# Values in two halves of their columns, VectorE's steps issued when ScalarE's results are made, and the mixer's gate behind six tiles of queries and keys

## The chip, the cores and the metric

The kernel runs on one core of a Trainium2 chip. The metric is the device time of one execution in microseconds (us), less is better. TensorE multiplies matrices, VectorE and ScalarE work element by element, GpSimd (POOL in the profile) does a few additions, SyncE (SP) issues the DMAs.

## The reference

Two layers of a decoder trunk over 512 positions of width 1024. Each layer has two half-step feed-forward blocks, between them a token mixer, and behind them a per-layer embedding. The change lies in the mixer:

```python
a_in = rms_norm(h, mix_pre_g[i])
proj = a_in @ w_in[i]
q, k, v, u = jnp.split(proj, [D_ATTN, 2 * D_ATTN, 3 * D_ATTN], axis=-1)
q = partial_rotary(...); k = partial_rotary(...)          # 8 heads of 64
attn = dilated_mixture_attention(q, k, v)                 # windows (128,1) (512,4) (2048,16)
ssm = s5_mixer(u, ...)                                    # 32 groups of 16 channels, 64 states
mixed = jnp.concatenate([rms_norm(attn, attn_norm_g[i]), rms_norm(ssm, ssm_norm_g[i])], axis=-1)
h = h + rms_norm(mixed @ w_out[i], mix_post_g[i])
# the end of s5_mixer:
y = jax.nn.gelu(y)
y = y * jax.nn.sigmoid(y @ w_glu + b_glu)
```

All of it is float32, and the sequence is one batch of 512 positions.

## The kernel before

Activations lie with channels on the 128 partitions and the 512 positions along the free axis. A product with weights is done in three passes of a rounded format: each operand is split into a high half (ScalarE copies it, which rounds) and a low half (VectorE subtracts), and `mm3` (line 632) multiplies high by high, high by low and low by high. The weights come as units of 128 x 1024 words, in the order that `weight_units` (line 84) lists; `splitter` (line 694) splits a unit ahead of its use, up to two ahead, and `take` (line 712) forces it if it is not there. Raw units are loaded three ahead by DMAs on SP's queue.

Every engine runs its instructions in the order in which the program issues them. That order is made by a planner: `Clock` (line 203) keeps a modelled time for each engine, and work off the main line is written as generators that yield the modelled time at which they want to go on. `ck.after(ns)` waits for so much modelled time after TensorE's, `ck.written(ap)` is the modelled time at which an area is written, `ck.ready` the time at which TensorE may read it, `ck.idle("DVE")` the time at which VectorE has nothing left. The main line issues matmuls; before each step (`step`, line 967) it lets all generators go on whose time has come. None of these is a wait of the hardware: they only set what stands before what in each engine's queue. Real waits are semaphores of the data.

The mixer is `mix` (line 1821). First six units (`HEAD`, line 49) are multiplied: four of u, the input of the state-space part, and the query and key tiles of the first two heads (a head pair, t = 0). Then the main line multiplies the values (lines 1886 to 1900): four units hold two blocks of 128 input channels each and all 512 value columns, and four PSUM banks, one for each block of 128 positions, gather over all units, so that no values are there before the end of the fourth. Then come the other six query and key tiles, two to a head pair, with the gate `glu` (line 1941) ahead of tile `GLU_AT` = 4 (line 51), which counts the two in `HEAD`: two tiles, the gate, four tiles. Then the output projection's state-space half, which needs the four normalised pairs `xs`, and its attention half, which needs all attention.

Beside the main line run: two lanes of `mixer` (line 1559), each with two of four octets of groups; `attention` (line 1778), at most three `block`s (line 1686) at a time, one per head pair and 128 queries, whose second product reads the values (line 1740 waits for all four); `parts` (line 1751), which makes the rounded halves of a head pair in six slots of the 36 (`NR`, line 43); `attended` (line 1798), which ends a head pair. The end of an octet is its GELU: ScalarE's Square, two VectorE steps, ScalarE's Tanh, a VectorE step, a split into two rounded slots (lines 1662 to 1673). `glu` waits in the planner until both lanes are done, does four tiles of matmuls, and issues after each at once Tanh, the VectorE product and the sum of squares; its `scale` then waits for the norm and makes the four pairs, with a pause for an idle VectorE behind each (line 1977).

The profile names nearly all instructions by the helper's line (616 and 629 for matmuls, 379 for the others), so rows are told apart by engine, operation and tile shape.

## Time and profile before

| | us |
|---|---|
| median of 3 runs | 2089.26 |
| lowest and highest | 2086.16, 2090.63 |
| the profiled execution | 2087.56 |
| its span, first to last instruction | 2085.8 |
| TensorE (PE) busy in it | 2030.9 |
| VectorE (DVE) busy | 1329.9 |
| ScalarE (ACT) busy | 807.0 |
| GpSimd (POOL) busy | 156.4 |

Busy time of a matmul is modelled, and matmuls overlap, so a busy TensorE is not one at its peak. PEclk is the clock that TensorE was granted, as a share of 2.4 GHz. A row of the timeline gives start, duration, engine, line, operation, what it writes and reads, shape and count; in brackets the idle time of the engine before it and what ended that. A row that merges several instructions shows the first one's shape.

### The profile page before, as it was taken

What the parts mean: (1) busy time and instruction counts of PE and PEld (TensorE: products, weight loads), DVE (VectorE), ACT (ScalarE), POOL (GpSimd) and SP (SyncE); (2) the same over time, 40 slices, a digit from 0 to 9 for tenths busy, and PEclk for the clock granted to TensorE, in tenths of its full rate; (3) what the DMA queues carried; (4) which work ended last, traced back from release to release, by engine and by line L of the source; (5) the groups of instructions that cost most, each with busy time, mean ns of one, the idle gap of its engine ahead of it and who ended that gap; (6) DMA issues with size and microseconds to landing.
All of it is one profiled execution on the core that took longest, in us unless ns stands there. A gap on an engine that the chain in (4) does not pass through costs nothing.

```text
span 2085.8 us, 30582 instructions
## 1 busy us (share of the span) xinstructions
PE 2030.9 (97%) x11864; PEld 1745.4 (84%) x11864; DVE 1329.9 (64%) x2516; ACT 807.0 (39%) x1406; POOL 156.4 (8%) x167
## 2 busy tenths in 40 slices
PE   7999999997999999999999999999999999999997
PEld 7888888985789888888998888889777988888897
DVE  6886654777778867445774444458877854445474
ACT  4422332444654333223553222234457543222253
POOL 0000000210220000001210000011011200000022
PEclk9999999999999999999999999999999999999999
DMA  5434342482233434424324233243812433323132
GB/s 162 126 95 147 107 140 91 155 183 63 81 114 114 155 105 131 136 64 159 112 78 145 63 114 107 76 158 122 183 52 71 141 113 98 114 71 123 60 131 72
DMA packets 118145, 236.29 MB, mean 113 GB/s; under 512 B 27120, under 2 KB 58480, under 8 KB 118000
## 3 DMA queue, kind: packets, MB, share of 16 engines
q1 hardware_dynamic: 118000, 234.34, 36.5%
q8 instruction: 93, 1.52, 0.3%
q14 instruction: 52, 0.43, 0.1%
HBM read 208.60 MB, written 25.69 MB: 112 GB/s over the span
## 4 chain that ended last, share of the span: by engine, by line
PE 88%; DVE 7%; ACT 2%; DMA 2%; issue 1%; SPq 0%; POOL 0%; DVEq 0%; ACTq 0%; POOLq 0%
PE ps_all L616 87%; DVE sb_all L379 4%; DVE sr_all L379 2%; PE ps_all L629 1%; ACT sb_all L379 1%; ACT sr_all L379 1%; DMA sb_all<-scratch_g 1%; DMA sb_all<-scratch_t 1%; SPq L379 0%; DMA sb_all<-xt 0%; DMA z<-scratch_t 0%; DVE z L379 0%; POOL sb_all L379 0%; ACT z L379 0%; DVEq L379 0%
## 5 line engine op out<-in xcount | busy, mean ns | idle before, releaser
L616 PE MATMUL ps_all<-sr_all 128*128 128x512 f32 (+1 forms) x7259 | 1421.6, 353 | 21.5 <-ACT sr_all L379 18.6
L616 PEld LDWEIGHTS ps_all<-sr_all 128*128 128x128 f32 x7259 | 1191.6, 190 | 209.0 <-ACT sr_all L379 20.4
L379 ACT ACTIVATE sr_all<-sb_all 128x1024 fp32r<-128x1024 f32 (+5 forms) x570 | 414.8, 744 | 593.1 <-DVE sb_all L379 432.1
L379 DVE TENSOR_TENSOR sr_all<-sb_all,sr_all 128x1024 fp32r<-128x1024 f32 (+4 forms) x458 | 422.1, 931 | 205.6 <-ACT sr_all L379 204.0
L616 PE MATMUL ps_all<-sr_all,z 128*128 128x512 f32 (+1 forms) x2757 | 547.4, 350 | 2.0 <-DVE sr_all L379 2.0
L616 PEld LDWEIGHTS ps_all<-sr_all,z 128*128 128x128 f32 x2757 | 452.0, 190 | 68.5 <-DVE sr_all L379 3.0
L379 DVE TENSOR_TENSOR sb_all<-ps_all,sb_all 128x512 f32<-128x512 f32 (+1 forms) x400 | 246.9, 622 | 325.1 <-PE ps_all L616 316.9
L379 ACT ACTIVATE sb_all<-sb_all 128x256 f32<-128x256 f32 (+3 forms) x388 | 187.6, 491 | 451.4 <-DVE sb_all L379 451.1
L379 POOL TENSOR_TENSOR sb_all<-sb_all 128x256 f32<-128x256 f32 (+3 forms) x159 | 152.7, 962 | 1924.5 <-ACT sb_all L379 1726.6
L379 DVE TENSOR_TENSOR sb_all<-sb_all 128x256 f32<-128x256 f32 (+7 forms) x605 | 238.3, 410 | 52.4 <-DMA scratch_t<-sb_all 37.2
L379 ACT ACTIVATE sb_all<-ps_all 128x512 f32<-128x512 f32 (+5 forms) x215 | 102.7, 492 | 165.2 <-PE ps_all L616 123.2
L379 DVE SCALAR_TENSOR_TENSOR sb_all<-sb_all 128x512 f32<-128x512 f32 (+3 forms) x194 | 115.1, 595 | 52.9 <-ACT sb_all L379 51.1
L379 DVE TENSOR_TENSOR z<-sb_all,z 128x1024 fp32r<-128x1024 f32 (+2 forms) x109 | 116.3, 1069 | 46.5 <-ACT z L379 46.2
L379 ACT ACTIVATE z<-sb_all 128x1024 fp32r<-128x1024 f32 (+2 forms) x109 | 100.4, 924 | 54.3 <-PE ps_all L616 37.7
L616 PEld LDWEIGHTS ps_all<-sb_all 128*64 128x64 f32 (+3 forms) x1364 | 76.6, 145 | 36.1 <-DVE sb_all L379 12.4
L616 PE MATMUL ps_all<-sb_all 128*64 128x128 f32 (+5 forms) x1364 | 88.8, 257 | 17.1 <-DVE sb_all L379 8.5
L379 DVE SCALAR_TENSOR_TENSOR sb_all<-sb_all,ps_all 128x256 f32<-128x256 f32 (+1 forms) x136 | 65.8, 485 | 4.4 <-ACT sb_all L379 2.8
L379 DVE TENSOR_SCALAR sb_all<-sb_all 128x32 f32<-128x32 f32 (+8 forms) x145 | 41.7, 296 | 29.6 <-POOL sb_all L379 17.0
L379 DVE SCALAR_TENSOR_TENSOR sr_all<-sb_all,sr_all 128x256 fp32r<-128x256 f32 x96 | 51.1, 543 | 0.4 <-ACT sr_all L379 0.4
L629 PE MATMUL ps_all<-sb_all 128*128 128x128 f32 x278 | 45.7, 279 | 5.0 <-DVE sb_all L379 3.8
L629 PEld LDWEIGHTS ps_all<-sb_all 128*128 128x128 f32 x278 | 33.2, 140 | 14.3 <-DVE sb_all L379 7.0
L379 DVE CUSTOM_DVE_ANT_0 sb_all<-ps_all,sb_all 128x512 f32<-128x512 f32 (+3 forms) x56 | 24.7, 491 | 16.5 <-PE ps_all L616 16.5
(36 smaller groups left out, 168.8 us busy)
## 6 DMA issues: line engine op xcount, KB each, us to landing
sb_all<-weights SPq DMA_DIRECT2D x263, 512.0 KB, 3.6
sb_all<-weights SPq DMA_DIRECT2D x96, 320.0 KB, 3.0
scratch_t<-sb_all SPq DMA_DIRECT2D x40, 256.0 KB, 3.8
scratch_h<-sb_all SPq DMA_DIRECT2D x80, 128.0 KB, 1.7
sb_all<-scratch_h SPq DMA_DIRECT2D x40, 256.0 KB, 5.5
sb_all<-scratch_t SPq DMA_DIRECT2D x16, 512.0 KB, 6.3
sb_all<-weights SPq DMA_DIRECT2D x32, 192.0 KB, 2.3
sb_all<-xt SPq DMA_DIRECT2D x16, 128.0 KB, 3.8
```

The costliest lines, as they stand in the source:

```text
L379: return f(*a, **k)
L616: self.nc.tensor.matmul(out, lhsT, rhs, start=start, stop=stop)
L629: self.nc.tensor.transpose(out, x, self.ident)
```

## The change

Values: a unit now holds four blocks of input channels and half of the value columns; for each half two units are taken, and each block of positions is summed up in one bank over eight steps of 256 columns and evicted at once. An attention block waits only for the half that its head pair needs. `GLU_AT` goes from 4 to 6: four query and key tiles stand ahead of the gate and two behind it, and the weight units are ordered to match. In the GELU, in `attended` and in the gate, VectorE steps that read a ScalarE result are issued when the planner holds it to be written. The gate's element-wise steps become a generator per tile. `scale` works in place, issues ScalarE's rounding of one tile before VectorE's subtraction of the tile before it, and has no pause.

```diff
-GLU_AT = 4
+GLU_AT = 6
@@ lay_out
         elif name == "w_in" and how == "v":
-            b = w[t * 2 * P:(t + 1) * 2 * P, 2 * DA:3 * DA].reshape(2, P, DA).transpose(1, 0, 2)
+            c = 2 * DA + t // 2 * HALF
+            b = w[t % 2 * 4 * P:(t % 2 + 1) * 4 * P, c:c + HALF].reshape(4, P, HALF).transpose(1, 0, 2)
@@ mixer
             self.act(gw, ps, AF.Square)
+            yield self.ck.written(gw)
             self.ts(gw, gw, 0.044715, 1.0, ALU.mult, ALU.add)
             self.tt(gw, ps, gw)
             self.act(gw, gw, AF.Tanh, scale=math.sqrt(2 / math.pi))
-            yield self.ck.after(500.0)
+            yield self.ck.written(gw)
             self.stt(self.b(g), gw, 1.0, ps, ALU.add, ALU.mult)
@@ block
-        while len(M["have"]) < 4:
+        while t // 2 not in M["have"]:
             yield self.ck.after(200.0)
-        yield self.ck.ready(*pt, *[self.b(x) for x in v])
+        yield self.ck.ready(*pt, *[self.b(x)[:, t * P:(t + 1) * P] for x in v])
@@ attended
         self.sumsq(self.b(M["sqa"]), ps, t == 0)
+        yield self.ck.written(self.r(h))
         self.stt(self.r(l), ps, g, self.r(h).bitcast(F32), ALU.mult, ALU.subtract)
@@ mix
-        bks = [self.bank() for _ in range(4)]
-        for j in range(4):
-            u, = self.take("w_in")
-            for kk in range(2):
-                k = 2 * j + kk
-                c = slice(kk * SEQ, (kk + 1) * SEQ)
-                for t in range(4):
-                    s = slice(t * P, (t + 1) * P)
-                    self.step(self.pb(bks[t]), (self.r(x["H"][k]), self.r(x["L"][k])), s,
-                              u[0][:, c], u[1][:, c], k, KT)
-            self.done()
-        for t in range(4):
-            self.act(self.b(v[t]), self.pb(bks[t]), scale=x["rt"][:, t:t + 1])
-            self.free(bks[t])
-            have.append(t)
+        for half in range(2):
+            u = self.take("w_in", 2)
+            for t in range(4):
+                bk = self.bank()
+                s = slice(t * P, (t + 1) * P)
+                for k in range(KT):
+                    c = slice(k % 4 * HALF, (k % 4 + 1) * HALF)
+                    self.step(self.pb(bk, HALF), (self.r(x["H"][k]), self.r(x["L"][k])), s,
+                              u[k // 4][0][:, c], u[k // 4][1][:, c], k, KT)
+                    if t == 3 and k % 4 == 3:
+                        self.done()
+                self.act(self.b(v[t])[:, half * HALF:(half + 1) * HALF], self.pb(bk, HALF), scale=x["rt"][:, t:t + 1])
+                self.free(bk)
+            have.append(half)
@@ glu
+        def gate(n, bk):
+            th = yield from self.sl.tget()
+            yield self.ck.written(self.pb(bk)) + 100.0
+            self.act(self.b(th), self.pb(bk), AF.Tanh, scale=0.25, bias=self.gain(i, "ssm_b_glu", n))
+            self.free(bk)
+            yield self.ck.written(self.b(th))
+            self.stt(self.b(ys[n]), self.b(th), 1.0, self.b(ys[n]), ALU.add, ALU.mult)
+            yield self.ck.written(self.b(ys[n]))
+            self.sumsq(self.b(sqs), self.b(ys[n]), not squares)
+            squares.append(n)
+            self.sl.put(th)
...
-                th = self.sl.get()
-                self.act(self.b(th), self.pb(bk), AF.Tanh, scale=0.25, bias=self.gain(i, "ssm_b_glu", n))
-                self.free(bk)
-                self.stt(self.b(ys[n]), self.b(th), 1.0, self.b(ys[n]), ALU.add, ALU.mult)
-                self.sumsq(self.b(sqs), self.b(ys[n]), n == 0)
-                self.sl.put(th)
+                gates.append(self.ck.spawn(gate(n, bk)))
...
         def scale():
+            while len(squares) < 4:
+                yield self.ck.after(100.0)
             yield from self.full_scale(sqs, 1.0 / (16 * DA), rs)
-            for n in range(4):
-                g = self.gain(i, "ssm_norm_g", n)
-                t = yield from self.sl.tget()
-                h = yield from self.rs.tget()
-                l = yield from self.rs.tget()
-                self.stt(self.b(t), self.b(ys[n]), g, self.b(rs))
-                self.split(self.r(h), self.r(l), self.b(t))
-                self.sl.put(t, ys[n])
-                xs.append((h, l))
-                yield self.ck.idle("DVE", 1000.0)
+            hl = []
+            def low(n):
+                h, l = hl[n]
+                self.tt(self.r(l), self.b(ys[n]), self.r(h).bitcast(F32), ALU.subtract)
+                self.sl.put(ys[n])
+                xs.append(hl[n])
+            for n in range(4):
+                hl.append((yield from self.rs.tgets(1, 1)))
+                y = self.b(ys[n])
+                self.stt(y, y, self.gain(i, "ssm_norm_g", n), self.b(rs))
+                self.act(self.r(hl[n][0]), y)
+                if n:
+                    low(n - 1)
+            yield self.ck.written(self.r(hl[3][0]))
+            low(3)
             self.sl.put(sqs, rs)
```

## Rows read from the trace of the kernel before

**Rows 1.** The page: busy time of each engine over the span.
```profile
PE 2030.9 (97%) x11864; PEld 1745.4 (84%) x11864; DVE 1329.9 (64%) x2516; ACT 807.0 (39%) x1406; POOL 156.4 (8%) x167
```

**Rows 2.** Windows: us, busy PE, PEld, DVE, ACT, POOL, PEclk, DMA, GB/s; between the mixers.
```profile
660.00:1460.00 800.00, 799.86 (x4268) 689.73 (x4267) 473.90 (x780) 275.37 (x443) 39.56 (x47) 1.00 0.36 114
```

**Rows 3.** Windows, same columns, two stretches of layer 0's mixer.
```profile
474.00:514.00 40.00, 26.36 (x267) 20.27 (x267) 33.84 (x86) 18.00 (x37) 3.32 (x2) 0.91 0.20 57
...
585.00:597.00 12.00, 10.34 (x74) 8.20 (x73) 9.04 (x22) 8.48 (x20) 2.77 (x3) 0.86 0.48 146
```

**Rows 4.** Windows, same columns, three stretches of layer 1's mixer.
```profile
1470.00:1476.00 6.00, 4.29 (x50) 3.47 (x50) 5.09 (x22) 3.78 (x11) 0.00 (x0) 1.00 1.08 246
...
1517.00:1533.00 16.00, 11.20 (x108) 8.23 (x108) 12.44 (x23) 9.61 (x16) 1.27 (x1) 0.97 0.04 14
...
1604.00:1620.00 16.00, 12.67 (x88) 9.28 (x87) 11.56 (x36) 12.69 (x30) 2.26 (x2) 0.82 0.27 86
```

**Rows 5.** Windows, same columns, two steps of 4 us in layer 0's hole.
```profile
486.00:490.00 4.00, 0.00 (x0) 0.00 (x0) 3.92 (x6) 1.27 (x3) 1.27 (x1) 0.71 0.01 4
490.00:494.00 4.00, 2.30 (x22) 2.26 (x24) 3.97 (x11) 1.24 (x2) 0.00 (x0) 0.50 0.00 0
```

**Rows 6.** Timeline of TensorE in that hole: the three longest waits.
```profile
491.70 3.32 PE L616 MATMUL ps_all<-sb_all 64*64 64x128 f32 x32 [8.46 <-DVE sb_all L379]
...
505.61 0.50 PE L616 MATMUL ps_all<-sr_all 128*128 128x512 f32 x1 [1.51 <-ACT sr_all L379]
...
510.44 0.50 PE L616 MATMUL ps_all<-sr_all 128*128 128x512 f32 x1 [1.13 <-ACT sr_all L379]
```

**Rows 7.** Timeline of TensorE: 24 matmuls of 512 and of 256 columns, and the next.
```profile
1561.09 5.60 PE L616 MATMUL ps_all<-sr_all 128*128 128x512 f32 x24
1566.54 0.63 PE L629 MATMUL ps_all<-sb_all 128*128 128x128 f32 x2
...
1451.76 3.04 PE L616 MATMUL ps_all<-sr_all,z 128*128 128x256 f32 x24
...
1454.64 1.60 PE L616 MATMUL ps_all<-sr_all 128*128 128x256 f32 x12
```

**Rows 8.** Timeline of VectorE: the first GELU step of an octet.
```profile
459.65 0.43 DVE L379 TENSOR_SCALAR sb_all<-sb_all 128x512 f32<-128x512 f32 x1 [1.10 <-ACT sb_all L379]
```

**Rows 9.** Timeline of VectorE: a weight unit's low half, a rotary.
```profile
479.19 1.22 DVE L379 TENSOR_TENSOR sr_all<-sb_all,sr_all 128x1024 fp32r<-128x1024 f32 x1
...
485.18 0.68 DVE L379 SCALAR_TENSOR_TENSOR sb_all<-ps_all,sb_all 128x512 f32<-128x512 f32 x1
...
485.79 0.72 DVE L379 STREAM_SHUFFLE sb_all<-ps_all 128x512 f32<-128x512 f32 x1
486.54 0.69 DVE L379 SCALAR_TENSOR_TENSOR sb_all<-sb_all 128x512 f32<-128x512 f32 x1
```

**Rows 10.** Timeline: last Tanh of the gate; low halves of the first, fourth pair.
```profile
525.58 0.69 ACT L379 ACTIVATE sb_all<-ps_all,sb_all 128x512 f32<-128x512 f32 x1 [0.22 <-PE ps_all L616]
...
537.62 0.69 DVE L379 TENSOR_TENSOR sr_all<-sb_all,sr_all 128x512 fp32r<-128x512 f32 x1 [0.70 <-ACT sr_all L379]
...
551.74 3.26 DVE L379 TENSOR_TENSOR sr_all<-sb_all,sr_all 128x512 fp32r<-128x512 f32 x4 [0.69 <-ACT sr_all L379]
```

**Rows 11.** Timeline of SP's queue in layer 0's hole: table loads, then weights.
```profile
473.92 8.04 SPq L379 DMA_DIRECT2D sb_all<-scratch_g  x8
...
482.06 43.10 SPq L379 DMA_DIRECT2D sb_all<-weights  x3
```

**Rows 12.** Timeline: second pair's scores, last octet's transposes, second pair's result.
```profile
499.77 2.36 PE L616 MATMUL ps_all<-sr_all 128*128 128x512 f32 x12
...
502.06 1.15 PE L616 MATMUL ps_all<-sb_all 64*64 64x64 f32 x32
...
524.21 0.67 ACT L379 ACTIVATE sr_all<-ps_all,sb_all 128x512 fp32r<-128x512 f32 x1
```

**Rows 13.** Timeline of TensorE at the end of layer 1's mixer.
```profile
1613.56 0.44 PE L629 MATMUL ps_all<-sb_all 128*128 128x128 f32 x2 [1.33 <-DVE sb_all L379]
```

More of the change, by code (lines that the diff above doesn't have):

```diff
@@ L1946, in glu @@
         ys = M["g"]
+        gates = []
+        squares = []
+        def gate(n, bk):
[9 more added lines that the diff above has]
+            self.sl.put(th)
         for t in range(2):
```

## Prediction

> **What bounds the kernel now.** I read the page first: TensorE has work for 97% of the span [rows 1], so time can only come from where TensorE has none, or runs at half clock, or from making its work shorter. Second I cut the span into long stretches with the view of windows: 660 to 1460 us holds 799.86 us of matmul in 800 [rows 2], and nothing can be won in such a stretch. The idle time lies in the two token mixers, roughly 430 to 660 us (layer 0) and 1455 to 1680 us (layer 1), which are also all that the diff touches. Third I cut the mixers at the places where the view of waits names long TensorE waits. Layer 0 has one large hole, 474 to 514 us, where 26.36 us of 40 are busy, so 13.64 us idle, and a small one, 585 to 597 us, of 1.66 us [rows 3]. Layer 1 has 1.71 us at 1470 to 1476, 4.80 us at 1517 to 1533 and 3.33 us at 1604 to 1620 [rows 4]. The idle time has a price behind it: after 486 to 490 without a matmul the granted clock is 0.50 in 490 to 494, the lower of its two levels, 1.2 GHz instead of 2.4 [rows 5]; 2.30 us of matmul ran there, of which half, 1.15 us, is lost. By the mean clocks of [rows 3] and [rows 4], (1 - clock) x busy gives at most 2.4 us for 474 to 514, 1.4 for 585 to 597, 0.3 for 1517 to 1533 and 2.3 for 1604 to 1620. These holes with their clock are 25.1 + 6.4 = 31.5 us, 1.5% of the span: a ceiling for the placement edits.
>
> Fourth I asked the timeline what ends each wait in the large hole [rows 6]: 8.46 us for VectorE (the state that the second pass of the state-space mixer multiplies with C), then 1.51 and 1.13 us for ScalarE (the halves of GELU outputs that the gate's matmuls read). VectorE is busy 3.92 and 3.97 us of 4 there [rows 5], so the hole is a chain of VectorE work with nothing queued on TensorE behind it: the gate is next in program order and it needs all four octets. On TensorE everything behind a waiting matmul waits too.
>
> **The change part by part.** *The gate behind six tiles.* Two query/key tiles (24 matmuls of 512 columns each) move from behind the gate to ahead of it, into the hole. 24 such matmuls start 1561.09 and end where the next starts, 1566.54: 5.45 us, 227 ns each [rows 7]. Two tiles are 10.9 us of cover for the 13.64 us in layer 0 and the 4.80 us in layer 1. They bring work to VectorE where it is full: per tile a rotary of 0.68 + 0.72 + 0.69 us and the low half of its weight unit at 1.22 us [rows 9], so 2 x (2.1 + 1.2) = 6.6 us. If all of it lands ahead of the octets' steps the gate moves back by 6.6 us and the cover is worth 4.3 us; if all lands behind, 10.9. I take the middle, 3.3 us of pushback, because the planner mixes them: 7.6 us in layer 0. In layer 1 the hole is smaller than the cover: 4.80 + 0.3 us at most, 0 at least; I take 4. The two weight loads move ahead of the gate's two loads on SP's queue, and there stand behind eight table loads that occupy it 8.04 us [rows 11]; the first weight load issues at 482.06, about where the moved tiles begin. Units are loaded three ahead, so I cost this at nothing; if that lead is gone, it is a wait of a few us inside the moved tiles, which the pushback's far end covers.
>
> What loses its cover: the norm behind the gate. From the last gate's Tanh at 525.58 to the first normalised pair is 537.62 + 0.69 = 538.3, 12.7 us, and the fourth is there at 552.4 [rows 10]. Four query/key tiles, 21.8 us, lay under that; now two do, 10.9 us. The rewritten scale step shortens the second part: it scales in place, has ScalarE round the next while VectorE subtracts the one before, and asks for no idle VectorE in between. From the first pair to the fourth 14.1 us pass now; eight VectorE steps of 0.69 us [rows 9, 10] are 5.5, the first step's 0.7 off is 4.8, so the fourth comes some 12.7 + 4.8 = 17.5 us after the Tanh. Against it stand 10.9 us of tiles, attention (twelve of its score matmuls take 2.36 us [rows 12]), and the first steps of the output projection, which need only the first pairs. I put a new wait of 2 us per layer there, between 0 and 17.5 - 10.9 = 6.6.
>
> *Values in two halves.* 96 matmuls of 512 columns become 192 of 256. 24 of 256 columns take 1451.76 to 1454.64, 2.88 us, 120 ns each [rows 7]. So 192 x 0.120 - 96 x 0.227 = 23.0 - 21.8 = +1.24 us a layer, +2.5 in all, all of it on TensorE and certain. The Trainium skill, "TensorE: Matmul & The Clock Gate", section "Back-to-back issue gap", speaks against this part: it says that in a stream of weight loads and matmuls the spacing is set by both, 131 ns at 512 columns and 81 at 128. The trace disagrees at 512 columns, 227 against 131 [rows 7]; by the page's two figures the loss would be at least (192 x 81 - 96 x 131) ns = 3.0 us a layer, an estimate, and the sum below would lose 3.5 us more. Two units are needed at once instead of one; the planner may split two ahead of use, and VectorE's and ScalarE's work is the same, so I cost that at nothing, up to one split (1.22 us) a layer if the second is late. Four more evictions go to ScalarE, busy 18.00 us of 40 even in the hole [rows 3]. The gain: one PSUM bank is held instead of four, and the first two head pairs can multiply with the values at half time, so their slots come free earlier. What it can save directly is the small waits near the values, 0 to 1.71 us in layer 1 [rows 4]; I take 0.5.
>
> *VectorE's steps when ScalarE's are made.* No hardware wait is added; instructions are only issued later, so that others stand ahead in VectorE's queue. Where VectorE stood still for ScalarE's Square it lost 1.10 us [rows 8], and the like for Tanh, in each of eight octets. These count only where VectorE is the one waited for, that is in the second octets in the holes, and there VectorE is already 98% full [rows 5]: nearest to zero, and I count nothing beyond the 7.6 us. A loss is possible where an issue slips to a later planner step; 0.5 us in each of the four octets at the holes would be 2 us.
>
> *The end of the mixers* (585 to 597, 1604 to 1620) is the last attention blocks with no projection left beside them: [rows 13] shows TensorE waiting 1.33 us for a softmax. The moved tiles let the third head pair's attention begin earlier, but the fourth pair's tiles stay where they are. 1.66 + 1.4 + 3.33 + 2.3 = 8.7 us at most, 0 at least; I take a third, 3.
>
> Sum: gains 7.6 + 4 + 0.5 + 3 = 15.1; losses 2.5 + 2 x 2 = 6.5; net 8.6 us faster. Against the profiled execution, 2087.56 us (its span 2085.8 and 1.8 around it), that is 2079.0; that execution lies 1.7 us under the median of 2089.26, and on the median it is 2080.7. I put 2080.
>
> **The rivals.** *The hole is filled whole.* VectorE's extra work falls behind the octets, the norm is covered, and the tail closes: the cover's 10.9 with 2.4 of clock, 5.1 in layer 1, 8.7 of tail, 1.7 at the values, less 2.5, is 26 us, 2063. For it: the cover nearly equals the idle time. Against it: VectorE's full queue.
>
> *The hole only moves.* What is won ahead of the gate is lost behind it: the pushback is the whole 6.6 us, so the holes give 4.3 + 2, each norm takes 3 and the values cost 2.5: -6.3 + 6 + 2.5 = +2, 2091. For it: the norm's chain, 12.7 us, is longer than the 10.9 us left over it [rows 7, 10].
>
> *Slower: the rounded slots run short.* There are 36 slots for the rounded halves (line 43). Ahead of the gate stand the input's 16, eight for four octets' GELU, two for the first head pair's result, six for each head pair in attention. With two pairs that is 38. In the kernel before only one pair stood there. Somebody waits until the second pair's attention is done. If that is the third pair, little is lost; if it is the last octet, the gate hangs on that attention: in the kernel before, from its scores at 499.77 to its result at 524.21, 24 us [rows 12], and some 5 us of GELU after, 529. TensorE's work ahead of the gate, which now ends at 510.44 [rows 6], is used up at 510.4 - 13.6 + 10.9 = 508, so it stands 529 - 508 = 21 us less the attention's matmuls, say 17, where 13.64 stood: +3.4 in layer 0, and +12 in layer 1, where 4.80 stood. With the values' 2.5 and the norm's 2 to 4 that is 2109 if it happens in both, 2097 in layer 0 alone. It decides from the point where the third pair's tiles end before the last octet's transposes. Against it: those run at 502.06 [rows 12], and at 493.6 without the wait of 8.46 us, while the second moved tile cannot end before 483.2 + 10.9 = 494.1. It is close, but the octet is more likely first.
>
> **How the numbers follow.** A measurement of this kernel tells about 0.2%, 4.2 us, from no change. Forecast, part of the hole filled, 2068 to 2085: 0.58, and 2080 as its time. Filled whole, below 2068: 0.07. Only moved, 2085 to 2093: 0.18. Slots short, above 2093: 0.17. So faster 0.65, same 0.18, slower 0.17. The range leaves out about one in ten on each side: from inside the filled case, 2065, to inside the slow one, 2097.
>
> **What would show it.** Right: the stretch that now is 474 to 514 holds query/key matmuls of 512 columns in place of the 8.46 us wait, the gate's first wait is below 3 us, values show 256-column matmuls at 120 ns, and the fourth normalised pair is ready within 18 us of the last gate's Tanh. Wrong on the norm: TensorE waits over 3 us for ScalarE or VectorE ahead of the output projection. Wrong on the slots: the last octet's Square comes long after its transposes, next to the second pair's result. Wrong on the tail: the waits for the last softmax stay. The forecast falls as a whole if VectorE, not TensorE's order, sets when the last octet ends.

## The result

The changed kernel takes 2066.03 us in the median (2063.90 to 2068.35), the kernel before, run beside it, 2089.95 us (2086.16 to 2091.18): a ratio of 0.9889, 95% interval 0.9872 to 0.9906, so 23.9 us less. I had forecast 2080 us, 9.3 us less. The time lies in my range (2065 to 2097) by 1 us, but 2 us below the band of my forecast, 2068 to 2085: it falls to "the hole is filled whole", to which I gave 0.07. The gain is two and a half times the forecast.

The page's busy times, to be set beside [rows 1]; the span is 2062.1 us:

```profile
PE 2025.4 (98%) x12056; PEld 1751.7 (85%) x12056; DVE 1327.8 (64%) x2516; ACT 807.7 (39%) x1414; POOL 157.3 (8%) x167
```

TensorE's idle time falls from 54.9 to 36.7 us (span less busy), and its busy time by 5.5 although the values cost more: clock won back (by the table below, 9.4 us lost to it in the mixers before, 3.2 now). Windows of the changed kernel in layer 0 (columns as in [rows 2]): the mixer up to the norm, the norm behind the gate, the tail, which is the last attention at the mixer's end. They answer to [rows 3].

```profile
460.00:534.00 74.00, 73.95 (x605) 61.02 (x602) 64.24 (x139) 43.85 (x84) 13.44 (x9) 1.00 0.37 109
534.00:549.00 15.00, 11.27 (x63) 7.88 (x61) 14.22 (x33) 9.17 (x23) 2.29 (x2) 0.89 0.01 2
...
580.00:584.00 4.00, 3.27 (x28) 3.10 (x27) 2.76 (x6) 1.02 (x3) 0.85 (x1) 1.00 0.99 346
```

And in layer 1, where the same gap behind the gate is the largest, for [rows 4]:

```profile
1552.00:1564.00 12.00, 8.46 (x45) 5.97 (x46) 11.62 (x29) 6.22 (x14) 1.70 (x2) 0.87 0.00 1
```

The hole of 13.64 us is gone: in 74 us TensorE stands for 0.05. In its place stand query and key matmuls with the gate's right behind them and no wait between, in the merged row that begins at 493.01 below. What is left are 3.73 us of waiting with (1 - 0.89) x 11.27 = 1.24 us of clock behind the gate (3.54 and 1.10 in layer 1), and 0.73 us in each tail. The waits behind layer 0's norm and tail are named in TensorE's timeline:

```profile
493.01 15.32 PE L617 MATMUL ps_all<-sr_all 128*128 128x512 f32 x69
...
535.87 0.65 PE L630 MATMUL ps_all<-sb_all 128*128 128x128 f32 x4 [0.78 <-POOL sb_all L380]
...
542.30 0.51 PE L617 MATMUL ps_all<-sr_all 128*128 128x512 f32 x1 [2.44 <-ACT sr_all L380]
...
580.90 0.65 PE L630 MATMUL ps_all<-sb_all 128*128 128x128 f32 x4 [0.73 <-POOL sb_all L380]
```

To compare layers I take SP's issue of the first three u stores as a landmark; in the kernel before, then in the changed one:

```profile
419.08 2.42 SPq L379 DMA_DIRECT2D scratch_u<-sb_all  x3
...
1450.71 2.41 SPq L379 DMA_DIRECT2D scratch_u<-sb_all  x3
```

```profile
417.89 2.43 SPq L380 DMA_DIRECT2D scratch_u<-sb_all  x3
...
1434.61 2.39 SPq L380 DMA_DIRECT2D scratch_u<-sb_all  x3
```

From landmark to landmark layer 0 took 1031.6 and takes 1016.7 us, 14.9 less; from the second landmark to the end layer 1 took 635.1 and takes 627.5, 7.6 less.

What I had not expected is in VectorE's timeline of the changed kernel. The last octet's low half is made at 499.13; in the kernel before it comes at 510.42, where the wait at 510.44 ends [rows 6]. The moved tiles put 6.6 us of work on VectorE, and still the octets of layer 0 end 10 us earlier from the landmark (81.2 instead of 91.3 us). Changed, then before:

```profile
499.13 0.69 DVE L380 TENSOR_TENSOR sr_all<-sb_all,sr_all 128x512 fp32r<-128x512 f32 x1 [1.03 <-ACT sr_all L380]
499.74 0.68 DVE L380 CUSTOM_DVE_ANT_0 sb_all<-ps_all,sb_all 128x512 f32<-128x512 f32 x1
```

```profile
500.54 0.69 DVE L379 CUSTOM_DVE_ANT_0 sb_all<-ps_all,sb_all 128x512 f32<-128x512 f32 x1 [1.66 <-PE ps_all L616]
...
510.42 0.69 DVE L379 TENSOR_TENSOR sr_all<-sb_all,sr_all 128x512 fp32r<-128x512 f32 x1 [0.70 <-ACT sr_all L379]
```

CUSTOM_DVE_ANT_0 at 512 columns is the second head pair's first softmax step: right behind the last octet in the changed kernel, ahead of it in the kernel before.

The time from the landmark to this low half is VectorE's busy time plus its idle time. Windows over it, VectorE's busy time being the fourth number, layer 0 and layer 1; before, then changed:

```profile
419.08:510.42 91.34, 77.68 (x756) 63.58 (x754) 72.52 (x171) 40.03 (x79) 9.11 (x6) 0.96 0.59 135
1450.71:1530.17 79.46, 73.08 (x736) 59.28 (x734) 66.22 (x150) 32.87 (x62) 6.94 (x6) 1.00 0.68 155
```

```profile
417.89:499.13 81.24, 81.19 (x867) 71.96 (x866) 70.19 (x157) 38.97 (x72) 10.30 (x7) 1.00 0.68 158
1434.61:1515.75 81.14, 81.14 (x866) 71.96 (x866) 70.20 (x158) 38.98 (x72) 10.25 (x7) 1.00 0.67 159
```

In layer 0 the idle time falls from 18.8 to 11.0 us, which is 7.8 of the 10.1 us, and the work ahead by 2.3. In layer 1 the idle time falls only from 13.2 to 10.9 us and the work ahead grows by 4.0, so there the octets end 1.7 us later than before; what layer 1 gains comes from the two tiles' cover and from the tail.

### The profile page after: what moved, and what is told of

Read it like the earlier page. It is cut to its first block, busy times and chain, and to the rows that moved or that the text cites. A ratio compares the mean times of both kernels' runs of the same rounds, so it can differ in the third digit from the quotient of the medians.

```text
span 2062.1 us, 30997 instructions
## 1 busy us (share of the span) xinstructions
PE 2025.4 (98%) x12056; PEld 1751.7 (85%) x12056; DVE 1327.8 (64%) x2516; ACT 807.7 (39%) x1414; POOL 157.3 (8%) x167
## 4 chain that ended last, share of the span: by engine, by line
PE 91%; DVE 5%; issue 1%; ACT 1%; DMA 0%; POOL 0%; SPq 0%; POOLq 0%; DVEq 0%; ACTq 0%
PE ps_all L617 90%; DVE sb_all L380 3%; DVE sr_all L380 2%; PE ps_all L630 1%; POOL sb_all L380 0%; ACT sr_all L380 0%; DMA sb_all<-weights 0%; ACT sb_all L380 0%; SPq L380 0%; DVE z L380 0%; DMA sb_all<-scratch_t 0%; POOLq L380 0%; DVEq L380 0%; ACTq L380 0%
## 5 line engine op out<-in xcount | busy, mean ns | idle before, releaser
L617 PE MATMUL ps_all<-sr_all 128*128 128x512 f32 (+2 forms) x7436 | 1429.6, 349 | 21.4 <-ACT sr_all L380 17.3
L380 DVE TENSOR_TENSOR sr_all<-sb_all,sr_all 128x1024 fp32r<-128x1024 f32 (+5 forms) x459 | 420.3, 926 | 197.6 <-ACT sr_all L380 196.2
L617 PE MATMUL ps_all<-sr_all,z 128*128 128x512 f32 (+1 forms) x2772 | 532.7, 346 | 0.0
L380 DVE TENSOR_TENSOR sb_all<-sb_all 128x256 f32<-128x256 f32 (+6 forms) x605 | 239.3, 411 | 48.7 <-DMA scratch_t<-sb_all 36.4
L630 PEld LDWEIGHTS ps_all<-sb_all 128*128 128x128 f32 x282 | 33.3, 139 | 10.8 <-POOL sb_all L380 5.0
```

The lines of the kernel that those rows point to most:

```text
L380: return f(*a, **k)
L617: self.nc.tensor.matmul(out, lhsT, rhs, start=start, stop=stop)
L630: self.nc.tensor.transpose(out, x, self.ident)
```

## The experiments

Theory A: the halves and the placed steps make the octets early, and the tiles fill what is left. Rival B: the tiles alone fill the hole. The table has every run, in the order of the text. Each ratio is to the kernel before run beside it, whose median lay between 2088.16 and 2090.47 us, so a difference of 2 us between rows is not told apart. The last three columns come from one profiled execution of each kernel. "Idle" is VectorE's idle time in the 30 us from 20 us behind the first landmark (windows); "end" the start of layer 0's last octet's low half, from the landmark; "lost" what TensorE lost in the 230 us behind each of the two landmarks, idle time plus (1 - clock) x busy over steps of 2 us.

| kernel | median us | ratio, 95% interval | idle | end | lost |
|---|---|---|---|---|---|
| before | 2089.95 | | 11.1 | 91.3 | 39.7 |
| changed | 2066.03 | 0.9889, 0.9872 to 0.9906 | 5.3 | 81.2 | 15.5 |
| e_tiles_only | 2109.06 | 1.0086, 1.0073 to 1.0100 | 10.9 | 113.9 | 62.1 |
| e_gate_at_4 | 2078.86 | 0.9946, 0.9933 to 0.9958 | 5.5 | 79.3 | 32.0 |
| e_no_halves | 2101.38 | 1.0052, 1.0039 to 1.0065 | 10.4 | 115.8 | 52.8 |
| e_no_placement | 2107.29 | 1.0082, 1.0068 to 1.0096 | 7.5 | 112.0 | 58.0 |
| e_halves_only | 2094.82 | 1.0031, 1.0021 to 1.0041 | 7.4 | 90.1 | 48.1 |
| e_placement_only | 2091.67 | 1.0016, 1.0007 to 1.0024 | 10.6 | 95.0 | 47.0 |
| e_tiles_held | 2107.80 | 1.0089, 1.0075 to 1.0102 | 10.8 | 97.3 | 61.0 |
| e_no_placement_held | 2099.30 | 1.0051, 1.0037 to 1.0064 | 7.4 | 92.7 | 50.4 |
| e_before_octets_first | 2092.80 | 1.0020, 1.0011 to 1.0029 | 11.1 | 89.0 | 48.8 |
| e_tiles_octets_first | 2103.02 | 1.0068, 1.0055 to 1.0081 | 10.8 | 96.1 | 57.3 |
| e_no_placement_octets_first | 2093.61 | 1.0023, 1.0013 to 1.0032 | 7.4 | 89.8 | 45.4 |
| e_no_halves_octets_first | 2085.37 | 0.9982, 0.9974 to 0.9991 | 10.2 | 95.4 | 35.1 |
| e_both_halves | 2086.02 | 0.9988, 0.9979 to 0.9997 | 7.7 | 109.9 | 42.0 |
| e_no_mixer_steps | 2095.74 | 1.0038, 1.0026 to 1.0051 | 7.4 | 111.5 | 42.9 |
| e_no_gate_steps | 2091.09 | 1.0014, 1.0005 to 1.0023 | 5.3 | 81.2 | 44.0 |
| e_gate_at_5 | 2071.44 | 0.9919, 0.9905 to 0.9932 | 6.0 | 81.6 | 21.1 |
| e_gate_at_5_then_6 | 2067.14 | 0.9901, 0.9887 to 0.9914 | 5.3 | 81.2 | 17.8 |
| e_gate_at_6_then_5 | 2064.61 | 0.9887, 0.9872 to 0.9902 | 5.3 | 81.3 | 14.5 |

### The three parts, one alone or one left out

The kernel before with the moved tiles alone:

```diff
-GLU_AT = 4
+GLU_AT = 6
```

> The kernel before, with the gate behind six query/key tiles and nothing else. Theory A (the octets end some 10 us earlier because head pair 0 can multiply with half the values and VectorE's steps are placed, and the tiles only fill what is left): without these two the octets aren't earlier, VectorE's extra 6.6 us push them back, and the old norm chain, 14.1 us from first to fourth pair, has two tiles fewer over it: 2083 to 2090 us. Theory B (the moved tiles alone fill the hole, and what else moves earlier follows from that): TensorE's wait for the last octet is under 3 us and the time is 2066 to 2076 us.

2109.06 us, 0.9% slower. Rival B falls, and theory A's number too: it is worse than a hole only partly filled. TensorE's waits in layer 0:

```profile
513.40 1.97 PE L616 MATMUL ps_all<-sb_all 64*64 64x64 f32 x32 [5.35 <-ACT sb_all L379]
...
562.30 0.50 PE L616 MATMUL ps_all<-sr_all 128*128 128x512 f32 x1 [2.62 <-ACT sr_all L379]
...
566.16 1.94 PE L616 MATMUL ps_all<-sr_all 128*128 128x512 f32 x3 [1.98 <-ACT sr_all L379]
```

The last octet's transposes start at 513.40, its low half comes 20 us later (533.36, against 7.2 us in the changed kernel). The waits from 562 on are the norm's.

The changed kernel with the gate at four again:

```diff
-GLU_AT = 6
+GLU_AT = 4
```

> The changed kernel with the gate behind four query/key tiles, as before; halves and placement stay. Theory A: the octets still end about 10 us earlier, so TensorE's hole ahead of the gate shrinks from 13.6 to about 4 to 6 us, and four tiles lie over the norm: 2068 to 2077 us. Theory B: the hole stays, 10 us or more, and the halves' price comes on top: 2084 to 2091 us.

2078.86 us: 11.6 of the 23.9 us come without a tile moved. Theory A's window was 2068 to 2077, so it is missed by 2 us, on its side. By the landmarks layer 0 took 1018.3 us, 13.3 less than before: of the 13.64 us of its hole 3.74 are left, as the window shows. Layer 1 took 639.2, 4.1 more: there the gate still waits 7.23 us for the last octet, whose low half starts at 1520.08, 82.3 us from the landmark, against 79.5 before. VectorE's idle time 20 to 50 us behind that landmark is less (5.5 against 8.8 us) and is lost again further on, so that stretch alone does not set the octets' end; why layer 1 behaves so, no run here shows.

```profile
474.00:514.00 40.00, 36.26 (x336) 29.02 (x335) 31.84 (x74) 22.01 (x42) 3.30 (x3) 0.96 0.26 77
```

```profile
1520.10 11.62 PE L617 MATMUL ps_all<-sr_all 128*128 128x512 f32 x39 [7.23 <-ACT sr_all L380]
```

This wait ahead of layer 1's gate is what the two moved tiles cover: they take layer 1 from 639.2 to 627.5 us.

The changed kernel without the halves (the unit's layout and the blocks' wait for all values go with it; the diff is cut):

```diff
-        for half in range(2):
-            u = self.take("w_in", 2)
+        bks = [self.bank() for _ in range(4)]
+        for j in range(4):
+            u, = self.take("w_in")
...
```

> The changed kernel with the values in whole columns again, as before; tiles and placement stay. Theory A: head pair 0's attention ends near 483 us again instead of 461, the last octet's GELU comes late, TensorE waits 5 us or more ahead of the gate in layer 0: 2074 to 2084 us. Theory B: the halves cost TensorE 2.5 us and give nothing, so the time is 2062 to 2065 us.

2101.38: beyond even theory A. And without the placed steps:

```diff
-            yield self.ck.written(gw)
...
-            yield self.ck.written(gw)
+            yield self.ck.after(500.0)
...
-        yield self.ck.written(self.r(h))
...
-                gates.append(self.ck.spawn(gate(n, bk)))
```

> The changed kernel without the placed steps: VectorE's and ScalarE's steps are issued where the kernel before issues them, in the octets, in the attention's result, in the gate and in its norm; tiles and halves stay. If the halves bring the octets forward (theory A, its first half), the last octet's low half is still near 499 us, and only the norm gets longer, by the 4.8 us that I counted for the scale step: 2068 to 2076 us. If the placement brings them forward, the last octet's low half is back near 510 us and TensorE waits ahead of the gate: 2076 to 2086 us.

2107.29, beyond both cases. Each part left out costs 13 to 41 us, so their worth doesn't add up; each must be in place for the others to pay. The next two show it from the other side, on the kernel before with the halves alone (the first of these two diffs, reversed) and with the placed steps alone (the second, reversed).

> The kernel before with the values in two halves alone. As I predicted, 2.5 us of matmul more and at most 1 us back: 2090 to 2093 us. If the early first half brings forward the first pair's attention (to 461 us from 483) and with it VectorE's later work, the wait of 8.46 us is under 5 and the time 2078 to 2085 us.

> The kernel before with the placed steps alone. Halves and placement together are worth 11.6 us with the gate where it was. If VectorE's standing still (1.10 us at each Square, the like at each Tanh) is what makes the octets late, placement has most of it: 2078 to 2084 us and TensorE's 8.46 us wait below 5. If placement counts for nothing there, as I predicted, 2087 to 2092 us.

Both are slower than before, by 0.3 and 0.2%, together with the gate at four they are 0.5% faster. The column "idle" tells why. VectorE's work is what layer 0's octets wait for, and VectorE stood idle 11.1 of 30 us in a stretch that ends 5 us ahead of the hole that I had looked at. Windows of this stretch, VectorE's busy time being the fourth number; before, placement alone, halves alone, changed:

```profile
439.10:469.10 30.00, 29.74 (x361) 24.09 (x361) 18.90 (x55) 12.19 (x25) 0.00 (x0) 1.00 0.84 215
```

```profile
439.40:469.40 30.00, 29.08 (x340) 23.56 (x339) 19.39 (x55) 11.70 (x25) 0.00 (x0) 1.00 0.70 183
```

```profile
440.10:470.10 30.00, 30.00 (x419) 26.88 (x418) 22.61 (x67) 14.29 (x34) 0.00 (x0) 1.00 0.84 217
```

```profile
437.90:467.90 30.00, 29.95 (x415) 26.63 (x415) 24.74 (x74) 13.69 (x33) 0.00 (x0) 1.00 0.85 218
```

The halves give 3.7 us, the placed steps on top of them 2.1, without them 0.5. With the halves alone it is of no use: up to the last octet VectorE is idle for 18.9 us, as long as before (18.8), because the time is lost again behind this stretch. What holds VectorE without the halves is seen in the timeline of e_placement_only: ScalarE stands 11.36 us, then has the values' four evictions in one row, and VectorE waits 3.55 us for a weight unit's high half that ScalarE makes behind them. In the changed kernel ScalarE's longest wait there is 4.35 us.

```profile
457.35 0.60 ACT L379 ACTIVATE sb_all<-ps_all 128x512 f32<-128x512 f32 x1 [11.36 <-PE ps_all L616]
...
460.52 2.42 ACT L379 ACTIVATE sb_all<-ps_all,sb_all 128x512 f32<-128x512 f32 x4
...
465.43 1.23 DVE L379 TENSOR_TENSOR sr_all<-sb_all,sr_all 128x1024 fp32r<-128x1024 f32 x1 [3.55 <-ACT sr_all L379]
...
469.98 0.69 DVE L379 TENSOR_TENSOR sr_all<-sb_all,sr_all 128x512 fp32r<-128x512 f32 x1 [2.73 <-ACT sr_all L379]
```

### Is it who comes first, or VectorE's lost time?

Two orders change when the octets are late: the third head pair takes its six rounded slots before the last octet takes its two (my rival), and the second pair's softmaxes come ahead of the octet's last steps. The first is taken away by

```diff
+        while t == 2 and len(M["took"]) < 4:      # in parts; an octet that has its slots adds to "took"
+            yield self.ck.after(200.0)
```

> The kernel before with the gate behind six tiles and one more line: the third head pair takes its six rounded slots only once all four octets have taken theirs. Theory S (the tiles alone are slower because the third pair takes the slots first and the last octet's GELU then waits for the second pair's attention): the last octet's GELU follows its transposes at once, its last step moves from 534 us to about 516, and the time falls from 2109 to 2076 to 2088 us, which is what my prediction's forecast, hole partly filled, would be worth without halves and placement. Theory T (the tiles' rotaries and low halves push VectorE's and ScalarE's queues back, whoever holds slots): the time stays above 2098 us.

> The changed kernel without the placed steps (2107 us) plus that one line. Theory S: 2070 to 2082 us, so that placement is worth 4 to 16 us by itself, most of the old difference of 41 us being the slots. Theory T, the queues: above 2096 us.

The first kernel is e_tiles_only with these lines, the second e_no_placement. In both the last octet ends 17 and 19 us earlier, so the kept slots do bring it forward; the time falls by 1.3 and 8.0 us only. Theory S had the event right and its price wrong. In e_tiles_held the waits moved behind the gate: 2.77 and 5.27 us for the norm at 547.68 and 560.28. The second order is taken away as well by

```diff
+            while t and len(M["gh"]) < 4:          # in attention, ahead of a pair's first block
+                yield self.ck.after(200.0)
```

> The kernel before plus one line: from the second head pair on, attention's blocks start only once all four octets are through GELU. Theory R (what decides is whether the second pair's softmaxes, 3.2 us of VectorE and their scores, get into the queues ahead of the last octet; in the kernel before they start at 500.54 us with the last low half behind them at 510.42): the last low half comes at about 505 us, the gate 5 us earlier, the hole shrinks by 3 to 6 us, and the attention that no longer runs beside the octets lies over the norm instead: 2078 to 2087 us. Theory T (the octets are late because VectorE stood still much earlier, for the values' four banks and for ScalarE's results): within 4 us of before, 2085 to 2093.

> The kernel before with the gate behind six tiles, slots kept for the octets, and the second pair's attention held until the octets are through. Theory R: the octets end near 508 us instead of 518, and the tiles then cover the hole: 2076 to 2090 us. Theory T: the octets end late all the same, TensorE waits behind them and behind the norm, and the time stays above 2096 us.

> The changed kernel without the placed steps, with the same two lines (slots kept, second pair held). Theory R: the last octet comes before the second pair's softmaxes as in the changed kernel, last low half near 503 us, and 2070 to 2084 us. Theory T: VectorE's standing still for ScalarE, some 3 us an octet, keeps the octets late, 2090 us or more.

> The changed kernel with the values in whole columns, the rounded slots kept for the octets and the second pair's attention held until the octets are through. If the halves help only because without them slots and second pair get ahead of the last octet, the time is 2064 to 2076 us. If VectorE's idle time early in the mixer (10.4 us instead of 5.2) is what counts, the last low half comes 5 us later than in the changed kernel and the time lies at 2078 to 2096 us.

The first has the second line alone, the others both. Theory R falls as the whole cause: each of the first three lies in theory T's window, and the fourth in that of VectorE's lost time, its octet 14 us later than in the changed kernel where I expected 5. In the first the octets end 2.3 us earlier than before, and it is 0.2% slower. The price of the two orders together is read from pairs of runs: 6.0 us of the tiles alone, 13.7 of e_no_placement, 16.0 of e_no_halves. What is left of the last two, 28 and 19 us over the changed kernel, was not taken apart further. In e_no_placement_octets_first much of it must be the norm, since the gate's steps are missing there, which alone cost 25 us (e_no_gate_steps). The lines have a price of their own, as the slower first kernel shows, and the changed kernel with both lines was not run, so these prices are rough. The first two kernels give a measure of the pushback too. With VectorE late, two tiles more ahead of the gate move the octet's end from 89.0 to 96.1, 7 us for 10.9 us of cover; with halves and placement (e_gate_at_4 to changed) from 79.3 to 81.2, 1.9 us.

### Inside the halves and inside the placement

The changed kernel, but the first pair's blocks wait for both halves; the values still use one bank at a time:

```diff
-        while t // 2 not in M["have"]:
+        while len(M["have"]) < 2:
```

> The changed kernel with one difference: a block of the first head pair multiplies with the values only when both halves are there; the values still use one bank at a time. If the early first half is what helps, VectorE's idle time 20 to 50 us after the first u store goes from 5.2 us back to 9 or more, the last low half comes near 508 us, and the time is 2082 to 2100 us. If the banks are, the idle time stays below 7 us and the time is 2064 to 2074 us.

2086.02, the early half's side; the idle time, 7.7 us, lies between the two cases. Of the 5.1 us of idle time from e_no_halves to the changed kernel about half goes with the banks and half with the first pair's attention finished early. But the last low half, expected near 508 us, comes at 529.62, 109.9 us from the landmark: VectorE does 91.1 us of work ahead of it instead of 70.2, so what counts here is mostly what gets into VectorE's queue ahead of the octet.

The changed kernel without the two placed steps in the octets:

```diff
             self.act(gw, ps, AF.Square)
-            yield self.ck.written(gw)
...
             self.act(gw, gw, AF.Tanh, scale=math.sqrt(2 / math.pi))
-            yield self.ck.written(gw)
+            yield self.ck.after(500.0)
```

> The changed kernel without the two placed steps in the octets (Square and Tanh are again followed at once by VectorE's step in the queue); attention's, the gate's and the norm's stay. If these two are what placement does for the octets, VectorE's idle time 20 to 50 us after the first u store is near 7.5 us as without any placement, the last low half comes after 504 us with the second pair's softmaxes ahead of it, and the time is 2085 to 2107 us. If they count for nothing, as I predicted, 2064 to 2070.

2095.74, as expected if they count: two lines are worth 29.7 us here. The octet's low half falls behind the second pair's softmaxes and starts 30.3 us later from the landmark than in the changed kernel. Of these, 21.2 us are work that VectorE does ahead of it (91.4 instead of 70.2 us) and 9.1 idle time:

```profile
507.87 0.69 DVE L380 CUSTOM_DVE_ANT_0 sb_all<-ps_all,sb_all 128x512 f32<-128x512 f32 x1
...
530.25 0.69 DVE L380 TENSOR_TENSOR sr_all<-sb_all,sr_all 128x512 fp32r<-128x512 f32 x1 [2.85 <-ACT sr_all L380]
```

The changed kernel with the gate's steps and the norm's `scale` as before:

```diff
-                gates.append(self.ck.spawn(gate(n, bk)))
+                th = self.sl.get()
+                self.act(self.b(th), self.pb(bk), AF.Tanh, scale=0.25, bias=self.gain(i, "ssm_b_glu", n))
...
+                yield self.ck.idle("DVE", 1000.0)
```

> The changed kernel with the gate and its norm as before; the placed steps in the octets and in attention stay. The octets stay early, last low half near 499 us; the norm's chain from the first to the fourth pair goes from 3.6 us back to about 14, of which the output projection's steps cover half: 3 to 8 us a layer longer, 2071 to 2082 us. If the gate's steps bear on the octets too, over 2085.

2091.09. The octets end at 81.2 as in the changed kernel, so these steps don't bear on them; my first case was right on that and far off on the price. TensorE waits 12 us for the norm in each layer:

```profile
536.64 0.50 PE L617 MATMUL ps_all<-sr_all 128*128 128x512 f32 x1 [2.21 <-ACT sr_all L380]
...
539.53 5.06 PE L617 MATMUL ps_all<-sr_all 128*128 128x512 f32 x14 [1.21 <-ACT sr_all L380]
551.59 1.95 PE L617 MATMUL ps_all<-sr_all 128*128 128x512 f32 x3 [7.00 <-ACT sr_all L380]
...
558.21 0.50 PE L617 MATMUL ps_all<-sr_all 128*128 128x512 f32 x1 [1.57 <-ACT sr_all L380]
```

and its clock falls to 0.66 in the stretch, (1 - 0.66) x 17.57 = 6.0 us more:

```profile
534.00:564.00 30.00, 17.57 (x81) 12.48 (x82) 19.66 (x44) 16.04 (x33) 1.28 (x1) 0.66 0.10 34
```

### Where the gate should stand

`GLU_AT = 5` in both layers, then `5, 6` and `6, 5` for layer 0 and layer 1:

```diff
-GLU_AT = 6
+GLU_AT = 5, 6
...
-            if j == GLU_AT:
+            if j == GLU_AT[i]:
```

> The changed kernel with the gate behind five query/key tiles, so that 5.45 us of tiles move from ahead of the gate to behind it. In layer 0 the gate at four waits 3.7 us for the octets, which one tile covers; in layer 1 it waits 7.2 us, of which one tile leaves about 2. The norm gap of 3.73 us and 1.24 us of clock per layer closes. The third pair's keys come behind the gate, so the tail gets some of its waits back, 0 to 3 us a layer. Sum: 10 us won on the norm, 2 lost in layer 1, 0 to 6 on the tails: 2058 to 2066 us. If the third pair's late keys cost the tail what the tiles cost with the gate at four, 2068 to 2074.

> The changed kernel with the gate behind five tiles in layer 0 and behind six in layer 1. From the traces: layer 0, first u store to first u store, took 1014.2 us with five and 1016.7 with six; layer 1 to the end took 635.4 and 627.5. If the layers don't touch one another this is 2.5 us faster than the changed kernel, 2062 to 2066 us. If layer 1 answers to where layer 0 ends, it can be anything up to 2072.

> The changed kernel with the gate behind six tiles in layer 0 and behind five in layer 1. Layer 1 with five took 635.4 us from its first u store to the end where layer 0 also had five, 627.5 with six. If that is layer 1's own, the time is 2070 to 2076 us; if layer 1's order answers to where layer 0 ends, 2060 to 2070.

2071.44, 2067.14 and 2064.61 us. None is told apart as faster than the changed kernel: the last one's interval, 0.9872 to 0.9902, overlaps the changed kernel's. In layer 0 five tiles close the norm's gap and open the tail again (in e_gate_at_5 TensorE waits 0.71, 0.56 and 0.68 us at 572.42, 574.83 and 577.33), as I had feared. Layer 1 with five took 635.4 us behind a layer 0 with five and 625.2 behind one with six, so it does answer to where layer 0 ends; why, no run here shows.

## Why the prediction was right and wrong

**Right**: the bound (TensorE, idle in two mixers only), the sign, and most of the tiles' worth. They take the kernel from 2078.86 to 2066.03; with each set against the kernel before run beside it that is 23.9 - 11.6 = 12.3 us, where my terms for cover, tail and norm gave 7.6 + 4 + 3 - 4 = 10.6. The hole holds query and key matmuls, the gate doesn't wait, and where I put them the signs came out: the values' 256 columns take at most 128 ns each, as this row of layer 1 shows (120 predicted), so their price is 192 x 0.120 to 0.128 less 96 x 0.227, 1.2 to 2.8 us a layer. The 3.0 us that I had worked out beside it from two figures of the Trainium skill ("TensorE: Matmul & The Clock Gate", section "Back-to-back issue gap") is just above that; its 131 ns at 512 columns stays at odds with the 227 of [rows 7].

```profile
1443.81 13.91 PE L617 MATMUL ps_all<-sr_all 128*128 128x256 f32 x109
```

**Wrong: "VectorE's steps when ScalarE's are made ... I count nothing", and "what it can save directly ... I take 0.5" for the halves.** This is the step that failed. Of these my sum has 2.0 us lost; measured with the gate at four they gain 11.6 us. That is 13.6 of the 15.3 us between my sum, 8.6, and the measured 23.9. I argued that VectorE is 98% full in the hole [rows 5], so nothing can be won there. Those are two steps of 4 us: in the whole stretch it was busy 33.84 of 40 us [rows 3]. And a full engine late in a chain asks when it began to be full. Of the 7.8 us of VectorE's idle time that layer 0 wins, 5.8 lie in 439 to 469 us, where TensorE stood for only 0.26 us, and 3.1 behind that, less 1.1 lost ahead of it; the 1.10 us that I had read there [rows 8] was one of many such stands. This holds for layer 0; in layer 1 the octets end 1.7 us later than before.

**Wrong in sign: the pushback of 3.3 us.** The two moved tiles themselves do push layer 0's octets back, by 1.9 us (e_gate_at_4 to changed), inside my bounds of 0 and 6.6. But its octets are there 10 us earlier than before, not 3.3 later. My own last sentence on what would overturn the forecast, that VectorE sets when the last octet ends, was the case; that it went to the good side, and left the forecast's sign standing, was luck.

**Mis-sized: the norm's wait, 2 us a layer.** It is 3.73 + 1.24 and 3.54 + 1.10. This was one of my signs for "wrong on the norm" (over 3 us), and the fourth pair is ready 24.3 us behind the last Tanh, where 18 was my sign of being right. From the last gate's Tanh to the first pair I had 12.7 us; in the changed kernel it is 542.97 - 522.28 = 20.7, because each link queues behind attention's work on ScalarE and VectorE:

```profile
522.28 0.69 ACT L380 ACTIVATE sb_all<-ps_all,sb_all 128x512 f32<-128x512 f32 x1
522.85 3.68 ACT L380 ACTIVATE sr_all<-sb_all 64x512 fp32r<-64x512 f32 x5
526.56 0.63 ACT L380 ACTIVATE sb_all<-sb_all 128x512 f32<-128x512 f32 x1
...
534.57 0.15 ACT L380 ACTIVATE sb_all<-ps_all 128x4 f32<-128x4 f32 x1
...
540.84 1.41 DVE L380 SCALAR_TENSOR_TENSOR sb_all<-sb_all 128x512 f32<-128x512 f32 x2
542.28 0.69 DVE L380 TENSOR_TENSOR sr_all<-sb_all,sr_all 128x512 fp32r<-128x512 f32 x1
...
545.84 0.69 DVE L380 TENSOR_TENSOR sr_all<-sb_all,sr_all 128x512 fp32r<-128x512 f32 x1
```

The rows are the last Tanh, the third pair's five `parts` steps ahead of the last product's square, the square, the column sums read behind six exponentials, and the first and the fourth pair. The other end of the term was too small as well: I gave the rewritten gate and `scale` 4.8 us of a chain, and together they are worth 25 us (e_no_gate_steps): from the first to the fourth pair it is now 3.6 us, not 14.1, in each layer's norm, and the clock that the longer waits cost comes on top.

**Mis-sized: the tail, 3 us.** Of the 8.7 us that I called the most, 0.73 us a layer are left, so some 7 are won.

**The rival "the hole is filled whole"**, 2063 us, is nearest to what came, and half of its mechanism did: the gate does not wait and the tail is nearly closed. Its third condition failed, the norm is not covered. That two errors of mine, the octets and the tail against the norm, leave the time near its figure is chance.

**The rival of the rounded slots** did not occur in the changed kernel: the last octet's transposes run from 491.93 to 493.08 and its Square follows at once.

```profile
493.19 0.60 ACT L380 ACTIVATE sb_all<-ps_all 128x512 f32<-128x512 f32 x1 [1.17 <-PE ps_all L617]
```

It does occur with the tiles alone and without the placed steps: with the slots kept (e_tiles_held and e_no_placement_held) the octet ends 17 and 19 us earlier. That e_tiles_only came out at the rival's 2109 us is not its proof: with the slots kept it is still 2107.8.

Open stays how the 29.7 us of the two lines in the octets divide. The trace divides the octet's delay, 21.2 us of work let ahead of it and 9.1 us of idle time; which order lets that work ahead, the slots or the second pair, and what either costs the kernel, no run here shows.

## What to carry to other kernels

Where an engine is full just ahead of a wait, go back along its queue, and split the time up to the late result into the engine's idle time and the work that stands ahead: either may be what makes it late. One stretch is not enough, since time won early can be lost again behind it, as with the halves alone and in layer 1. Changes that guard the same chain don't add up; run them together and one left out at a time, since one alone can be slower where all are faster. A step whose result many wait for should not be queued behind one that waits for another engine, and a wait that is moved should be priced with the clock that it costs.

## What was not expected of the hardware

The share of the clock. In the changed kernel the mixers lose 3.2 us to it beside 12.3 of idle time, before 9.4 beside 30.3, with the tiles alone 21.4 beside 40.7. The loss does not follow the idle time alone: it is 11.3 beside 20.7 in e_gate_at_4 and 14.6 beside 42.6 in e_tiles_octets_first. In the stretch at 0.66 above, several waits follow one another; that this is what makes the loss large was not tested.
